# Exchanging two neighbouring stores in the DMA order of a matmul-and-subtract kernel

## The chip, the cores and the metric

The kernel runs on one core of a Trainium2 chip. The metric is device time in microseconds of one execution. The kernel before has a median of 210.92 us in four runs (210.59 to 211.15). Times inside a run are counted from the start of the profiled span, which is about 2 us shorter than the measured time of that same run. A transfer is spread over 16 DMA engines and leaves 16 landing records in the trace; "it lands" means the last of them, unless the first is named.

## The reference

```python
batch, m, k, n = 16, 512, 1024, 768
def reference(x, weight, sub_value):          # all float32
    return (np.matmul(x, weight) - sub_value).astype(np.float32)
```

The kernel sees it as 8192 rows of x by 1024, cut into 64 m tiles of 128 rows. Traffic with memory is 87 MB: 33.6 MB of x, 3.1 MB of weight, 25.2 MB of sub_value in, and 25.2 MB of result out.

## The kernel before

Every transfer is issued by the sync engine (SP), in the order of one list. A row ('x', 24, 8) loads m tiles 24 to 31 of x, 's' loads sub_value, 'o' stores the result. x has a ring of 16 slots; sub_value and the result share a ring of 32, and the subtraction works in place.

```python
SEGMENTS = [(0, 1), (1, 7)] + [(at, 8) for at in range(8, 64, 8)]
NX, NSO = 16, 32
TRANSFERS = [
    # ... cut: x and sub_value up to tile 15, all of the weight
    ('x', 16, 2), ('x', 18, 6), ('s', 16, 8),
    ('x', 24, 8), ('o', 0, 1), ('o', 1, 7), ('s', 24, 8), ('x', 32, 8), ('s', 32, 8), ('x', 40, 8),
    ('o', 8, 8), ('o', 16, 8), ('s', 40, 8), ('x', 48, 8), ('s', 48, 8), ('x', 56, 8),
    ('o', 24, 8), ('o', 32, 8), ('s', 56, 8), ('o', 40, 8), ('o', 48, 8), ('o', 56, 5),
    ('o', 61, 2), ('o', 63, 1),
]
```

What a row waits for, cut to the lines that matter. These waits stand on SP, which goes through its list in order:

```python
if kind == "x" and need:      # the slots' former tiles must have been cast
    waits.append((counter["cast"], max(cast_at[t] for t in need)))
    # ... cut
if kind == "s":               # the slots' former results must have landed in memory
    for t in need:
        waits.append(landed["o", t])
        # ... cut
if kind == "o":               # the tiles must have been subtracted
    waits.append((counter["finish"], max(finish_at[t] for t in need)))
    # ... cut
sem, value = lane((kind, at))  # the first semaphore whose former transfers are known to be over
```

A tile goes through ScalarE (cast to 16 bits), TensorE or VectorE (transposition), TensorE (16 matmuls of 128x384), and VectorE (the subtraction). The results of the matmuls have three buffers, so the matmuls of tile t need the subtraction of tile t - 3.

## Time and profile before

| | before |
|---|---|
| time, median of 4 | 210.92 us |
| span of the profiled run | 208.9 us |
| TensorE busy | 196.7 us, 94% |
| DMA engines' time in the transfers' queue | 97.7% |
| 49 to 186 us: TensorE busy, and rate of transfers | 136.72 of 137 us, 430 GB/s |

Two resources are full at once. Two more places bear on the argument and were not shown in it. First, TensorE's timeline of before at 186 us (start, duration, engine, line, what):

```profile
185.83 0.81 PE L198 MATMUL po_b<-w_sb,xtp_b 128*128 128x384 f16 x4
186.48 0.27 PE L335 MATMUL pt_b<-ident,x_b 128*128 128x128 f32 x1
186.75 0.81 PE L198 MATMUL po_b<-w_sb,xtp_b 128*128 128x384 f16 x4
```

Groups of four matmuls otherwise follow one another every 0.76 us; here the step is 0.92, a gap of 0.16 us that no list of waits names. VectorE's line for the subtraction of tile 56 ends 0.05 us before those matmuls (185.74 + 0.96 = 186.70, the first of three in the line):

```profile
185.74 2.69 DVE L417 TENSOR_TENSOR so_ring<-po_b,so_ring 128x768 f32<-128x768 f32 x3 [3.35 <-DMA so_ring<-in_sub_value_dram]
```

The second place is the last two stores of before, by size and time from issue to landing:

```profile
out_dram<-so_ring SPq DMA_DIRECT2D x1, 768.0 KB, 7.0
out_dram<-so_ring SPq DMA_DIRECT2D x1, 384.0 KB, 5.3
```

The last store, 384 KB, needs 5.3 us. Moving 384 KB at 430 GB/s takes 0.9.

### The profile page before, as it was taken

How to read it: one execution, taken by the hardware profiler on the slowest of the kernel's cores; microseconds unless marked ns; L12 is line 12 of the kernel's file. 1: busy time of each engine (PE TensorE's matmuls, PEld its weight loads, DVE VectorE, ACT ScalarE, POOL GpSimd, SP SyncE). 2: the span in 40 equal slices, each digit the busy share in tenths (PEclk: the TensorE clock that was granted, in tenths of full speed). 3: DMA queues.
4: the chain of work that ended last, by engine and by line, in shares of the span. 5: the costliest groups of instructions: out<-in, count | busy, mean ns of one | idle time of the engine just before them, and what ended most of it. 6: DMA issues, size and time to landing. Idle time of an engine off the chain costs nothing.

```text
span 208.9 us, 2614 instructions
## 1 busy us (share of the span) xinstructions
PE 196.7 (94%) x1234; PEld 75.4 (36%) x700; DVE 127.8 (61%) x224; ACT 108.8 (52%) x113; POOL 1.0 (0%) x7
## 2 busy tenths in 40 slices
PE   6999799989999999999999999999999999999950
PEld 0234244333434434433443443343344344334310
DVE  2323316955993995596499299369749929943330
ACT  4364768507664671762844767173584655525300
POOL 1000000000000000000000000000000000000000
PEclk9999999999999999999999999999999999999996
DMA  6999999999999999999999999999999999999992
GB/s 238 406 426 433 440 420 436 449 431 430 433 458 414 353 446 445 446 414 411 475 419 422 438 414 438 461 425 422 431 447 397 436 442 438 414 438 442 411 417 119
DMA packets 5620, 87.08 MB, mean 417 GB/s; under 512 B 624, under 2 KB 624, under 8 KB 2032
## 3 DMA queue, kind: packets, MB, share of 16 engines
q1 hardware_dynamic: 5616, 87.03, 97.7%
q8 instruction: 1, 0.02, 0.0%
q14 instruction: 3, 0.02, 0.0%
HBM read 61.87 MB, written 25.17 MB: 417 GB/s over the span
## 4 chain that ended last, share of the span: by engine, by line
PE 72%; DMA 18%; SPq 4%; ACT 1%; issue 1%; DVE 0%
PE po_b L198 65%; DMA x_ring<-in_x_dram 18%; PE pt_b L335 7%; SPq L298 3%; SPq L262 1%; ACT xt_b L348 0%; DVE so_ring L417 0%; ACT x_b L317 0%; SPq L553 0%; ACT x16p_b L317 0%; SPq L138 0%
## 5 line engine op out<-in xcount | busy, mean ns | idle before, releaser
L198 PE MATMUL po_b<-w_sb,xt_b 128*128 128x384 f16 x704 | 126.0, 326 | 0.3 <-ACT xt_b L348 0.2
L417 DVE TENSOR_TENSOR so_ring<-po_b,so_ring 128x768 f32<-128x768 f32 x64 | 60.4, 956 | 58.6 <-PE po_b L198 37.4
L348 ACT COPY xt_b<-pt_b 128x1024 f16<-128x1024 f16 x44 | 44.5, 1012 | 64.2 <-PE pt_b L335 63.2
L368 DVE STREAM_TRANSPOSE xtp_b<-x16p_b 32x256 f32<-32x256 f32 x144 | 62.7, 435 | 3.3 <-ACT x16p_b L317 1.1
L198 PE MATMUL po_b<-w_sb,xtp_b 128*128 128x384 f16 x320 | 61.4, 326 | 1.0 <-DVE xtp_b L368 0.9
L397 PEld LDWEIGHTS <-xt_b 128*128 128x128 f16 x352 | 34.4, 98 | 57.7 <-issue 53.6
L317 ACT CAST x_b<-x_ring 128x1024 f16<-128x1024 f32 x46 | 47.2, 1048 | 4.3 <-DMA x_ring<-in_x_dram 4.3
L335 PE MATMUL pt_b<-ident,x_b 128*128 128x128 f32 x184 | 47.6, 274 | 1.6 <-ACT x_b L317 1.4
L335 PEld LDWEIGHTS pt_b<-ident,x_b 128*128 128x128 f32 x184 | 25.3, 141 | 46.0 <-issue 41.3
L317 ACT CAST x16p_b<-x_ring 128x1024 f16<-128x1024 f32 x18 | 18.8, 1046 | 16.8 <-DMA x_ring<-in_x_dram 16.8
L397 PEld LDWEIGHTS <-xtp_b 128*128 128x128 f16 x160 | 15.7, 98 | 19.9 <-issue 17.8
L265 DVE CAST w_sb<-so_ring 128x768 f16<-128x768 f32 x8 | 4.1, 556 | 11.4 <-DMA so_ring<-in_weight_dram 11.4
L198 PE MATMUL po_b<-idle_x,idle_w 128*128 128x512 f16 x26 | 8.8, 495 | 1.7 <-POOL idle_x L178 1.7
L348 ACT COPY xtp_b<-pt_b 128x1024 f16<-128x1024 f16 x2 | 2.0, 1012 | 2.1 <-PE pt_b L335 2.1
L317 ACT ACT_TABLE_LOAD x1 | 1.3, 1283 | 0.9 <-SPq L138 0.9
L427 PEld LDWEIGHTS <-idle_w 128*128 128x128 f16 x4 | 0.4, 99 | 1.7 <-POOL idle_x L178 1.7
L187 DVE TENSOR_TENSOR ident<-along,across 32x32 f32<-32x32 f32 x4 | 0.7, 183 | 0.1
L179 DVE MEMSET ones<- 128x32 f32 x1 | 0.1, 85 | 1.0 <-SPq L138 1.0
L178 POOL MEMSET idle_x<- 128x512 f16 x1 | 0.5, 528 | 0.0
L499 ACT CAST stub<-ident 128x1 f16<-128x1 f32 x2 | 0.4, 195 | 0.0
L184 DVE STREAM_TRANSPOSE across<-along 128x32 f32<-128x32 f32 x1 | 0.2, 212 | 0.0
L476 POOL MEMSET mark<- 128x1 f32 x1 | 0.1, 99 | 23.6 <-ACT xtp_b L348 23.6
(7 smaller groups left out, 1.0 us busy)
## 6 DMA issues: line engine op xcount, KB each, us to landing
so_ring<-in_sub_value_dram SPq DMA_DIRECT2D x7, 3072.0 KB, 24.2
x_ring<-in_x_dram SPq DMA_DIRECT2D x5, 4096.0 KB, 23.8
out_dram<-so_ring SPq DMA_DIRECT2D x6, 3072.0 KB, 29.2
x_ring<-in_x_dram SPq DMA_DIRECT2D x2, 2048.0 KB, 27.0
so_ring<-in_weight_dram SPq DMA_DIRECT2D x4, 768.0 KB, 8.2
x_ring<-in_x_dram SPq DMA_DIRECT2D x1, 3072.0 KB, 28.6
out_dram<-so_ring SPq DMA_DIRECT2D x1, 2688.0 KB, 26.5
x_ring<-in_x_dram SPq DMA_DIRECT2D x2, 1024.0 KB, 24.8
```

Of the source, the lines that this page charges most:

```text
L178: pool.add(lambda: nc.gpsimd.memset(idle_x, 0.0), then=count("idle"))
L187: dve.add(lambda here=here: nc.vector.tensor_tensor(out=ident[here, here], in0=along[here], in1=across[here], op=mybir.AluOpType.is_equal, ...
L198: return nc.tensor.add_instruction(mybir.InstMatmult(name=nc.get_next_instruction_name(), engine=full.engine, ins=list(full.ins), outs=lis ...
L262: sp.add(lambda st=st, at=at: nc.sync.dma_start(out=st, in_=w_c[at]), then=(sem, 16))
L265: lambda at=at, r=r, st=st: nc.vector.tensor_copy(out=w_sb[:, at, r], in_=st[:, r]),
L298: sp.add(lambda here=here, there=there: nc.sync.dma_start(out=here, in_=there), waits, (sem, 16))
L317: act.add(lambda: nc.scalar.copy(out=to, in_=x_in), waits, count("cast"))
L335: pe.add(lambda: nc.tensor.transpose(words, from_, ident), waits, count("turn") if last else None)
L348: act.add(lambda: nc.scalar.copy(out=to, in_=pt_b[:, b]), waits, count("evac"))
L368: dve.add(lambda: nc.vector.transpose(xt[b * Q : (b + 1) * Q, :, a * Q : (a + 1) * Q], x16[a * Q : (a + 1) * Q, :, b * Q : (b + 1) * Q],), ...
L397: pe.add(lambda weights=weights: nc.tensor.ldweights(weights, tile_position=(0, 0)), [w for w in waits if w[0] in ready])
L417: dve.add(lambda: nc.vector.tensor_tensor(out=o, in0=po[:, :, :NS], in1=o, op=mybir.AluOpType.subtract), [landed["s", mi], (counter["mul"] ...
```

## The change

The store of tiles 1 to 7 goes ahead of the store of tile 0. The intent is that the large store starts as soon as it can; the bytes are the same.

```diff
-    ('x', 24, 8), ('o', 0, 1), ('o', 1, 7), ('s', 24, 8), ('x', 32, 8), ('s', 32, 8), ('x', 40, 8),
+    ('x', 24, 8), ('o', 1, 7), ('o', 0, 1), ('s', 24, 8), ('x', 32, 8), ('s', 32, 8), ('x', 40, 8),
```

## The prediction

> **What bounds the kernel now.** I read the page first for engine shares and the chain, then the DMA section, then the sync engine's timeline and waits around the two stores, and last what waits for the data that those stores gate. From the page, busy shares of a 208.9 us span, the DMA row in 40 slices, and the chain that ended last:
>
> ```profile
> PE 196.7 (94%) x1234; PEld 75.4 (36%) x700; DVE 127.8 (61%) x224; ACT 108.8 (52%) x113; POOL 1.0 (0%) x7
> ...
> DMA  6999999999999999999999999999999999999992
> ...
> PE 72%; DMA 18%; SPq 4%; ACT 1%; issue 1%; DVE 0%
> PE po_b L198 65%; DMA x_ring<-in_x_dram 18%; PE pt_b L335 7%; SPq L298 3%; SPq L262 1%; ACT xt_b L348 0%; DVE so_ring L417 0%; ACT x_b L317 0%; SPq L553 0%; ACT x16p_b L317 0%; SPq L138 0%
> ```
>
> The reader is to see two things. First, the chain is a transfer of x (18% of the span, in order of time the piece from 9.99 to 48.47 us) and then TensorE alone, from 49 us to the last subtraction at 201.26 us. Second, the DMA engines are full throughout as well: 87.08 MB at a mean of 417 GB/s. So the kernel has two near-bounds. A change of the order of transfers can only show if it changes what TensorE waits for after 49 us, or moves bytes after the end of the matmuls. After 50 us the matmul row's list of waits, asked for that stretch alone, has one entry:
>
> ```profile
> PE po_b L198 <- ACT xt_b L348: 0.2, 1, 0.2
> ```
>
> (columns: total us, times, longest). TensorE is idle for 0.2 us of the last 150 us of matmuls. There is nothing to win by feeding it better after 50 us; there is only something to lose.
>
> Now the stores themselves. The sync engine's timeline from 54 to 96 us (start, duration, what):
>
> ```profile
> 54.22 0.33 SPq L298 DMA_DIRECT2D x_ring<-in_x_dram  x1
> 54.59 0.91 SPq L298 DMA_DIRECT2D out_dram<-so_ring  x2
> 55.81 0.34 SPq L298 DMA_DIRECT2D so_ring<-in_sub_value_dram  x1
> 70.44 0.33 SPq L298 DMA_DIRECT2D x_ring<-in_x_dram  x1
> 81.54 0.33 SPq L298 DMA_DIRECT2D so_ring<-in_sub_value_dram  x1
> 94.80 0.33 SPq L298 DMA_DIRECT2D x_ring<-in_x_dram  x1
> ```
>
> These are x tiles 24 to 31, the two stores (one merged row), sub_value 24 to 31, x 32 to 39, sub_value 32 to 39, x 40 to 47. The two stores go out back to back at 54.59 and 55.07. Neither waits for a subtraction: the loading of x 24 to 31 ahead of them had waited for a cast until 54.22. Their sizes and landings, from the DMA issues of 54.5 to 55.5 us:
>
> ```profile
> out_dram<-so_ring SPq DMA_DIRECT2D x1, 2688.0 KB, 26.5
> out_dram<-so_ring SPq DMA_DIRECT2D x1, 384.0 KB, 20.6
> ```
>
> So tile 0 lands at 54.59 + 20.6 = 75.2 us and tiles 1 to 7 at 55.07 + 26.5 = 81.5 us. The one thing that waits for either is the load of sub_value 32 to 39, which overwrites the same slots of the ring. The sync engine's waits between 60 and 90 us:
>
> ```profile
> SPq L298 <- ACT x_b L317: 14.3, 1, 14.3
> SPq L298 <- DMA out_dram<-so_ring: 6.3, 1, 6.3
> SPq L59 <- DMA out_dram<-so_ring: 4.4, 1, 4.4
> ```
>
> After issuing x 32 to 39 (done at 70.77) it waits 4.4 us in a separate wait (line 59) for tile 0, to 75.2, then 6.3 us at the load itself for tiles 1 to 7, to 81.5. Only the later of the two landings matters.
>
> **What the Trainium skill says.** "DMA: Bandwidth & Descriptors", section "Queues, rings and completion order", says that each DMA engine consumes descriptors in ring order, and that one issuing engine has one ring on each of the 16. This case's trace agrees: all big transfers are in one queue (q1, 97.7% of the engines' time), and in the packet records each engine finishes its 32768-byte packets of x 24 to 31, then moves its 3072-byte packets of tile 0, then its 21504-byte ones of tiles 1 to 7. The landing records (last of 16 engines) follow the order of issue: x at 74.20, tile 0 at 75.16, tiles 1 to 7 at 81.52, sub_value 24 to 31 at 88.75, x 32 to 39 at 98.47, sub_value 32 to 39 at 105.73. The same page's "Anatomy of one DMA" says that DMA engines do not wait on semaphores, the issuing sequencer does. The waits above, on SP's queue, agree. So to exchange the two issues is to exchange two neighbours in a first-in first-out line.
>
> **The change part by part.**
> It adds and removes no instruction. The number of bytes, packets and their sizes stay; the two rows of the queue change places.
>
> 1. Issue. Tiles 1 to 7 now go out first and wait for the subtraction of tile 7, which tile 0 did not need. That subtraction is long done: the subtraction of tile 8 began at 46.14 us, when its sub_value landed (46.05), and the vector engine goes in order, so tile 7 was done at least 8.4 us before 54.59. Tile 0 behind it needs no wait any more. An already met wait costs no time that the trace shows: the two issues take 0.91 us together now, and I expect 0.91 again. Cost 0.0 us; sub_value 24 to 31 is again issued at 55.8.
>
> 2. Landing. Tile 0's share of the queue is 75.16 - 74.20 = 0.96 us (384 KB at 430 GB/s gives 0.91). Tiles 1 to 7 therefore land about 0.96 us earlier, at 80.6 (26.0 us after an issue at 54.59), and tile 0 lands last at about 81.5 (26.5 us after 55.07), 6.3 us later than now. The later of the two stays at 81.5, since the sum of bytes ahead of it is the same; I allow 0.3 us either way for which of the 16 engines is last (one transfer's landings spread over 2.3 to 2.7 us).
>
> 3. The gate. Tile 0's wait is still the first in program order, so the separate wait grows from 4.4 to about 10.8 us, and the one at the load (6.3 us) is met on arrival and vanishes. 4.4 + 6.3 = 10.7 before, 10.8 after. The load of sub_value 32 to 39 is issued at 81.5 to 81.9, at most 0.1 us later for passing two instructions after the event instead of one.
>
> 4. What that load is worth. When issued at 81.54 it stands behind x 32 to 39, which lands at 98.47. So a delay of the issue by a few tenths does not move its landing at 105.7. And it isn't needed then: the subtraction of tile 32 starts at 113.03 (I count back eight rows from the one at 137.33, which waited 4.66 us for sub_value 40 to 47 landing at 137.24), 7.3 us later. Off the path: 0.0 us.
>
> 5. The semaphores. The program gives each transfer the first free semaphore. By reading that logic, tile 0's and tiles 1 to 7's (the seventh and the ninth) are exchanged, both are free again at the same later point, and every later transfer keeps its own. No wait is added at the end.
>
> Sum: 0.0 + 0.0 + 0.0 us on the path, so 210.76 us stays; I write 210.8.
>
> **The rivals.** (a) The first store is held up by tile 7 and holds the queue behind it. For it: SP goes in order, and sub_value 24 to 31 behind it lands at 88.75, with its first use at 89.19, only 0.44 us later. Against it: the 8.4 us of margin in step 1. Even a hold-up of 1 us would not reach TensorE: the late sub_value at 137.33 stalled the vector engine for 4.66 us, and the matmul row shows no wait for it. It would make 210.8 to 211.
> (b) The last landing moves, since small packets now come at the end: a lone late engine could hold the gate. For it: the spread of 2.3 to 2.7 us. Against: 7.3 us of slack in step 4, and the line of x 32 to 39 before it. The load could be issued some 7 us late and still be in time, by estimate. It makes 210.8.
> (c) It gets faster, since the large store starts 0.96 us sooner. For it: DMA is at nine tenths everywhere. Against: nothing waits for tiles 1 to 7 without tile 0, and the end is set by TensorE. A gain would have to come from another run of chance: 210.6.
> (d) The switch from loads to stores costs differently with a large packet first. Tile 0's packets take 0.121 us for 3072 bytes (25.4 GB/s an engine), tiles 1 to 7's 0.799 us for 21504 (26.9): in either order the sum is the same, and a tenth of a microsecond at 75 us would be absorbed as above.
>
> **Range and chances.** The three runs of before lie between 210.59 and 211.15, so 0.56 us is the scatter of one and the same kernel. As every step gives zero, the range is that scatter with a little more for another chip or hour: 210.2 to 211.4. Within 2% means 206.5 to 215.0; no rival comes near either end. Chance of same 0.985; slower 0.01, for a queue effect that I cannot see here; faster 0.005.
>
> **What would show each step.** Step 1: two issues from about 54.6, together 0.9 us, no wait for the vector engine. Step 2: 2688 KB landing about 26 us after issue, 384 KB about 26.5 (20.6 before). Step 3: the separate wait of the sync engine for a store about 10.8 us, the 6.3 us one gone, the sub_value load issued at 81.5 to 81.9. Step 4: the landing of sub_value 32 to 39 at 105.7 within some tenths, the subtraction of tile 32 at about 113.0, and a chain still of x, then TensorE. It would be wrong if the two stores were issued later than 55.5, if the later of the two landed after 83 us, or if matmuls after 50 us showed waits for a subtraction.

## The result

The changed kernel takes 210.98 us (210.84 to 211.06, four runs), the kernel before 210.92. The ratio is 1.0003, with an interval of 0.9986 to 1.0021: the same. The instructions of TensorE, VectorE, ScalarE and GpSimd are the same ones in the same order; only the two neighbours in SP's list differ.

SP's timeline of the changed kernel, from 54 us to the load of sub_value 32 to 39:

```profile
54.42 0.33 SPq L298 DMA_DIRECT2D x_ring<-in_x_dram  x1
54.79 0.91 SPq L298 DMA_DIRECT2D out_dram<-so_ring  x2
56.01 0.34 SPq L298 DMA_DIRECT2D so_ring<-in_sub_value_dram  x1
70.64 0.33 SPq L298 DMA_DIRECT2D x_ring<-in_x_dram  x1
81.80 0.33 SPq L298 DMA_DIRECT2D so_ring<-in_sub_value_dram  x1
```

Everything is where it was, 0.2 to 0.3 us later throughout, because already x 24 to 31 went out 0.2 us later (54.42 against 54.22), ahead of the first changed instruction. The two stores by size and time to landing, and SP's waits between 60 and 90 us (total, times, longest):

```profile
out_dram<-so_ring SPq DMA_DIRECT2D x1, 2688.0 KB, 26.0
out_dram<-so_ring SPq DMA_DIRECT2D x1, 384.0 KB, 26.5
```

```profile
SPq L298 <- ACT x_b L317: 14.3, 1, 14.3
SPq L59 <- DMA out_dram<-so_ring: 10.8, 1, 10.8
```

Tile 0 now lands last, 26.5 us after issue instead of 20.6. The separate wait has grown from 4.4 to 10.8 us, and the 6.3 us wait at the load itself is gone. The load goes out 11.16 us after the one of x before it, against 11.10 before (81.54 - 70.44).

The chain of the page looks quite different, and that is a trap. Shares of the span by engine:

```profile
PE 51%; DMA 40%; ACT 3%; DVE 1%; issue 1%; POOL 0%; SPq 0%; POOLq 0%; DVEq 0%; ACTq 0%
```

DMA has gone from 18% to 40% in a kernel that takes as long. The chain in order of time, 140 to 188 us, shows the new way that it takes (start, duration, what):

```profile
140.40 31.17 DMA out_dram<-so_ring
...
171.58 14.43 DMA so_ring<-in_sub_value_dram
...
186.11 0.97 DVE so_ring L417
...
187.12 0.81 PE po_b L198 x4
```

The store of tiles 24 to 31 lands, the load of sub_value 56 to 63 follows it into the same slots, tile 56 is subtracted, and the matmuls of tile 59 begin. That was so before as well, with the gap of 0.16 us shown above. After, the gap is 0.33 (187.12 against the 186.79 of the regular step), and now the timeline names it:

```profile
187.12 0.81 PE L198 MATMUL po_b<-w_sb,xtp_b 128*128 128x384 f16 x4 [0.17 <-DVE so_ring L417]
```

The chain follows the one thing that came last. Where two come within some tenths of a microsecond of each other, it tips from one to the other and carries 22% of the span with it. The exchange did not tip it: after_again below is the changed kernel, unedited, and its page has yet another chain:

```profile
PE 75%; DMA 13%; DVE 6%; SPq 3%; issue 1%; DVEq 0%
```

### The profile page after: what moved, and what is told of

Read it like the earlier page. It is cut to its first block, busy times and chain, and to the rows that moved or that the text cites. A ratio compares the mean times of both kernels' runs of the same rounds, so it can differ in the third digit from the quotient of the medians.

```text
span 209.2 us, 2614 instructions
## 1 busy us (share of the span) xinstructions
PE 196.1 (94%) x1234; PEld 75.4 (36%) x700; DVE 127.8 (61%) x224; ACT 108.9 (52%) x113; POOL 1.0 (0%) x7
## 4 chain that ended last, share of the span: by engine, by line
PE 51%; DMA 40%; ACT 3%; DVE 1%; issue 1%; POOL 0%; SPq 0%; POOLq 0%; DVEq 0%; ACTq 0%
PE po_b L198 46%; DMA x_ring<-in_x_dram 19%; DMA out_dram<-so_ring 15%; DMA so_ring<-in_sub_value_dram 7%; PE pt_b L335 5%; ACT xt_b L348 1%; ACT x_b L317 1%; DVE so_ring L417 1%; POOL idle_x L178 0%; SPq L298 0%; POOL idle_w L177 0%; POOLq L553 0%; ACT x16p_b L317 0%; DVEq L59 0%; ACTq L59 0%
## 5 line engine op out<-in xcount | busy, mean ns | idle before, releaser
L317 ACT CAST x16p_b<-x_ring 128x1024 f16<-128x1024 f32 x18 | 18.8, 1046 | 17.1 <-DMA x_ring<-in_x_dram 17.1
L198 PE MATMUL po_b<-idle_x,idle_w 128*128 128x512 f16 x26 | 8.2, 469 | 1.7 <-POOL idle_x L178 1.7
```

Of the source, the lines that this page charges most:

```text
L198: return nc.tensor.add_instruction(mybir.InstMatmult(name=nc.get_next_instruction_name(), engine=full.engine, ins=list(full.ins), outs=lis ...
L317: act.add(lambda: nc.scalar.copy(out=to, in_=x_in), waits, count("cast"))
```

## The experiments

All are made from the changed kernel, and all ratios are to the kernel before. Letters of theories run on through the experiments: A is that the transfers are one first-in first-out line in which an issue is free as long as the line has work; E is that this line sets the end, F that TensorE does.

**after_again.** The changed kernel, unedited.

> The changed kernel again, on the chip that the next three share, to have its scatter beside theirs. Both theories: 211.0 us, ratio to the kernel before 0.998 to 1.002. If the small difference of the first measurement (210.98 against 210.92) were real, the ratio would stay above 1.000 in all rounds; I expect it to go either way.

Measured: 210.78 us, before 210.78; ratio 1.0005 (0.9991 to 1.0018). Nothing to explain. Both kernels moved by 0.1 to 0.2 us between sessions, more than the 0.06 us by which they had differed.

**gate_mid.** How late may the gate of sub_value 32 to 39 (SP's wait for the landing of both stores) open?

```diff
-    ('x', 24, 8), ('o', 1, 7), ('o', 0, 1), ('s', 24, 8), ('x', 32, 8), ...
+    ('x', 24, 8), ('o', 1, 7), ('s', 24, 8), ('o', 0, 1), ('x', 32, 8), ...
```

> Tile 0's store goes one place further back, behind the load of sub_value 24 to 31. Theory A (the transfers are a first-in first-out line, and an issue is free as long as the line has work ahead of it): tile 0 lands at about 88.9 us instead of 81.6, the load of sub_value 32 to 39 is issued at about 89 instead of 81.8, but it stands behind x 32 to 39 (landing 98.5) all the same and lands at about 105.9 as now. Time 211.0, within 0.3. Rival B (the later a gate opens, the later its load lands): landing 7.3 us later, at 113, just when it is needed, and x 40 to 47 unchanged; up to 0.5 us more.

Measured: 210.9 us, ratio 1.0003 (0.9988 to 1.0019). From SP's timeline:

```profile
70.92 0.33 SPq L298 DMA_DIRECT2D x_ring<-in_x_dram  x1
89.06 0.33 SPq L298 DMA_DIRECT2D so_ring<-in_sub_value_dram  x1
```

The load goes out at 89.06 instead of 81.80, and by the trace's landing records it lands at 105.9, as in the changed kernel. Its 7.3 us of later issue were spent standing in a line that was 7.3 us shorter. A holds, B falls.

**gate_late.** Tile 0's store goes behind x 32 to 39, so that the gate opens only when the line has run empty.

```diff
-    ('x', 24, 8), ('o', 1, 7), ('o', 0, 1), ('s', 24, 8), ('x', 32, 8), ('s', 32, 8), ...
+    ('x', 24, 8), ('o', 1, 7), ('s', 24, 8), ('x', 32, 8), ('o', 0, 1), ('s', 32, 8), ...
```

> Tile 0's store goes two more places back, behind x 32 to 39. Theory A: it lands last in the line, at about 98.6, and only then the load of sub_value 32 to 39 goes out, when the line is empty; that leaves a hole of about 2 us in the transfers (the first load of the kernel, on an empty line, landed its first bytes about 2.9 us after issue, of which about 1.2 are its own moving), so sub_value 32 to 39 lands at about 108, and all later transfers 1.5 to 2.5 us later. Sub_value 56 to 63, which the tile-59 matmuls already wait for by 0.2 to 0.3 us, comes later by as much. Time 212.5 to 213.5, ratio 1.007 to 1.012. Rival C (TensorE sets the time after 49 us and a late transfer is absorbed by slack): 211.0.

Measured: 215.58 us, ratio 1.0232 (1.0216 to 1.0248). C falls: nothing absorbs it. The direction is that of A, the size is 4.8 us where I had given 1.5 to 2.5. Stretches of 5 us of this run (time, busy of each engine, clock, DMA share, GB/s):

```profile
90.00:95.00 5.00, 5.00 (x34) 1.77 (x18) 4.83 (x11) 2.90 (x3) 0.00 (x0) 1.00 0.93 399
95.00:100.00 5.00, 5.00 (x34) 1.94 (x18) 2.61 (x5) 1.04 (x1) 0.00 (x0) 1.00 0.47 143
100.00:105.00 5.00, 5.00 (x35) 2.17 (x20) 2.89 (x5) 4.71 (x5) 0.00 (x0) 1.00 0.83 344
```

In the changed kernel the middle stretch moves 410 GB/s. The store landed on the first of the 16 DMA engines at 96.0 and on the last at 98.7; the wait is for the last, and the next load, issued at 98.77, lands on the first engine at 107.9 and on the last at 108.8. Less its own 7.3 us of moving, the last engine stood still for 2.8 us and the first for 4.6. I had sized the hole for an engine that finishes with the last. The load is 2.9 us late by its last landing, and x 40 to 47 behind it 4.3 us (119.9 against 115.6): another 1.4 us, which go with slowed packets (26 of those of x 40 to 47; by the packet records they lengthen its moving by 1.1 us on the mean engine), told under s24_first. The last landing is 4.6 us later than in the changed kernel.

**hold15.** The rival (a) of the prediction at full size: the first store waits for a later tile.

```diff
-  waits.append((counter["finish"], max(finish_at[t] for t in need)))
+  waits.append((counter["finish"], 16 if at == 1 else max(finish_at[t] for t in need)))
```

> The first store is held until the subtraction of tile 15 instead of tile 7 (ends at about 63.5 us instead of before 46), so the two stores and the load of sub_value 24 to 31 are issued at about 63.5 to 64.8 instead of 54.7 to 55.9, a hold-up of 8.9 us of the issuing engine. Theory A: the line still has x 24 to 31 before it until 74.3, so the landings stay as they are (80.7, 81.6, 88.9) within some tenths; 211.0 us, within 0.3. Rival D (an issue held up holds up what comes behind it, my rival a at full size): landings about 8.9 us later, sub_value 24 to 31 at about 97.8, tile 27 waits and the time grows by several us, to 214 or more.

Measured: 211.06 us, ratio 1.0008 (0.9993 to 1.0023). The issues of 63 to 65 us and their times to landing:

```profile
so_ring<-in_sub_value_dram SPq DMA_DIRECT2D x1, 3072.0 KB, 24.4
out_dram<-so_ring SPq DMA_DIRECT2D x1, 2688.0 KB, 17.1
out_dram<-so_ring SPq DMA_DIRECT2D x1, 384.0 KB, 17.6
```

The large store goes out 8.9 us later (63.68 against 54.79) and needs 8.9 us less (17.1 against 26.0). D falls.

**hold19.** As hold15 with 20 in place of 16, so that the hold outlasts the work in the line.

> The first store is held until the subtraction of tile 19, which ends at about 76.7 us, after x 24 to 31 has landed (74.3) and the line is empty. Theory A: the line stands still from about 72 to 74 until the first bytes of the store, about 2 us after 76.7; all landings from the stores on come 4 to 5 us later (stores at about 85 and 86, sub_value 56 to 63 at about 190), and the matmuls of tile 59 wait for that long. Time 214.5 to 216.5, ratio 1.017 to 1.026. Rival C (slack absorbs it): 211.0. Rival D (a hold-up counts in full from 54.7 on, 22 us): above 220.

Measured: 217.55 us, ratio 1.0324 (1.0309 to 1.0339). C and D fall; of A the mechanism holds and the size is again too small. Five microseconds of this run in which nothing moved:

```profile
72.00:77.00 5.00, 5.00 (x34) 1.86 (x18) 4.85 (x9) 2.98 (x4) 0.00 (x0) 1.00 0.00 0
```

By the landing records tile 0's store is 4.5 us late (86.3 against 81.7), as expected, and sub_value 32 to 39 4.9; x 40 to 47 is 5.7 us late, with slowed packets again, and the last landing 6.2.

Both late experiments lengthen the line, so both E and F allow them. The next runs tell E and F apart.

**tail_plain, tail_pe6, tail_pe12, tail_pe24.** TensorE's work is lengthened near the end, with the transfers as they are. tail_plain is the control and has the change of LOOP alone: TensorE's program is a loop of ten rounds of six tiles, and with nine the last six tiles are written out, so that one of them can be changed.

```diff
-LOOP = (4, 6, 10)
+LOOP = (4, 6, 9)
+  for _ in range(24 if mi == 62 and c == 0 and r == 0 else 0):     # 6, 12 or 24
+      pe.add(lambda weights=weights: loaded_matmul(
+          po[:, 0, :NS], weights, w_sb[:, 0, 0, :NS], start=True, stop=True), waits)
+      waits = []
```

> Control for the next two: the last six tiles of TensorE's loop are written out, nothing else. Both theories: 211.0 us, within 0.3.

> As tail_plain, with 6 more matmuls of 0.163 us before those of tile 62 (their result is overwritten, the outputs stay right): TensorE ends 0.98 us later. Theory E (the line of transfers, full to the end, sets the end: the last store is issued at 202.5 and its landings follow those of the stores before it): the line has work until about 206.9, so the last landing stays at 207.8; 211.0 us, within 0.3. Theory F (the chain as the profile tells it, TensorE sets the end): 212.0.

> As tail_plain, with 12 more matmuls before those of tile 62, so TensorE ends 1.95 us later. Theory E with a slack of about 2.9 us: 211.0, within 0.3. Theory F, or a slack below 1.5: 211.5 to 212.9.

> As tail_plain, with 24 more matmuls of 0.163 us before those of tile 62: TensorE ends 3.9 us later and the last store is issued at about 206.4. Theory E: the line empties at about 207 (the store of tiles 61 and 62 is issued at about 203.8 and lands by about 207), and the last store lands about 3.3 us after its issue, at about 209.7 instead of 207.8; so 212.5 to 213.2. Theory F: 214.9.

| | us, median | ratio (interval) | last subtraction starts | last store: issue to landing |
|---|---|---|---|---|
| tail_plain | 210.85 | 0.9994 (0.9981 to 1.0007) | 201.50 | 5.3 |
| tail_pe6 | 210.86 | 1.0006 (0.9991 to 1.0021) | 202.63 | 4.0 |
| tail_pe12 | 210.84 | 1.0003 (0.9989 to 1.0017) | 203.37 | 3.4 |
| tail_pe24 | 211.81 | 1.0052 (1.0039 to 1.0065) | 205.44 | 2.3 |

The last two stores of tail_pe12 and of tail_pe24, by size and time to landing:

```profile
out_dram<-so_ring SPq DMA_DIRECT2D x1, 768.0 KB, 5.1
out_dram<-so_ring SPq DMA_DIRECT2D x1, 384.0 KB, 3.4
```

```profile
out_dram<-so_ring SPq DMA_DIRECT2D x1, 768.0 KB, 3.2
out_dram<-so_ring SPq DMA_DIRECT2D x1, 384.0 KB, 2.3
```

TensorE can end almost 2 us later and the time doesn't move; the last store just stands less long behind others. With 3.94 us (205.44 - 201.50) the time grows by 0.96, so the slack of TensorE at the end is about 3.0 us. F falls. My size for tail_pe24 was off, and the time lies below the range that I had given: I had taken 3.3 us for a store on an empty line, from the first load of the kernel, and it needs 2.3.

**short_s56.** The line is made shorter, with TensorE's work as it is. The result is wrong (relative error 0.25): tiles 60 to 63 subtract stale data.

```diff
+            if kind == "s" and at == 56:
+                here, there = here[:, :4], there[:, :4]
```

> Wrong result on purpose: the last load of sub_value brings tiles 56 to 59 only, 1.57 MB less (3.65 us of the line at 430 GB/s), and the tiles 60 to 63 subtract what lies in the ring. TensorE has the same work. Theory E (the line of transfers sets the end, TensorE ends with about 2.9 us of slack, from the 3.9 us delay that cost 1.0): the last landing moves forward until the last store lands 2.3 us after its issue (as with the 24 added matmuls); with the matmuls of tile 59 no longer waiting, about 0.3 us more. Time 207.4 to 208.4, ratio 0.984 to 0.989. Theory F (TensorE sets the end): at most those 0.3 us, 210.6.

Measured: 207.87 us, ratio 0.9864 (0.9849 to 0.9879). The last two stores:

```profile
out_dram<-so_ring SPq DMA_DIRECT2D x1, 768.0 KB, 3.2
out_dram<-so_ring SPq DMA_DIRECT2D x1, 384.0 KB, 2.3
```

The last subtraction starts at 201.65, no earlier than in the changed kernel (201.63), and yet the time is 2.9 us shorter: the slack that the added matmuls had measured. The load is shorter by 3.65 us of moving; the last 0.7 are kept by TensorE, which now does set the end, as the last store's bare 2.3 us show. E holds from both sides.

One thing has to be added about the end of the line. Before, the last store lands on the first of the 16 DMA engines at 204.91 us and on the last at 207.59, and after 204 us few engines still move anything (DMA share and GB/s are the last two columns):

```profile
204.00:210.00 6.00, 0.00 (x0) 0.00 (x0) 0.00 (x0) 0.00 (x0) 0.00 (x0) 0.56 0.20 81
```

On the first engine the store needs 2.66 us from its issue, against 2.10 on the idle line of tail_pe24 (206.43 to 208.53, the last engine at 208.70). So most of TensorE's 3.0 us of slack is the backlog of the engines that finish last; against the engine that finishes first it is about 0.6 us, by estimate. What sets the end is the line of the latest engines. Why some run late was not tested.

**s24_first.** Both stores go behind sub_value 24 to 31.

```diff
-    ('x', 24, 8), ('o', 1, 7), ('o', 0, 1), ('s', 24, 8), ('x', 32, 8), ...
+    ('x', 24, 8), ('s', 24, 8), ('o', 1, 7), ('o', 0, 1), ('x', 32, 8), ...
```

> The load of sub_value 24 to 31 goes ahead of both stores. Two questions. First, the gate opens at about 89 instead of 81.6, as with tile 0's store alone moved; the line hides it: no cost. Second, the stall at the first change from loads to stores (the packets of x 24 to 31 took up to 1.9 us instead of 1.21, some 1.5 us of the line): if it comes from loads of x being overtaken by stores, it is gone or moves to the end of sub_value 24 to 31. If it goes, the line and the time are 1.0 to 1.5 us shorter, 209.5 to 210; if it only moves, 211.0 within 0.3. I expect that it moves.

Measured: 211.05 us, ratio 1.0014 (1.0002 to 1.0027). So this order costs 0.14%, by the interval 0.27% at the most, and whether that little is real stays open; the stall has only moved. In the changed kernel 28 of the 34 packets of x that start between 68 and 73 us take longer than 1.3 us, up to 2.78, where 1.21 is usual; in s24_first none does, and there 29 of the 50 packets of sub_value that start between 75 and 80 us take more than 1.0 us, up to 1.94, where 0.91 is usual. Windows of s24_first around it (DMA share and GB/s are the last two columns):

```profile
74.00:76.00 2.00, 2.00 (x15) 0.73 (x7) 1.93 (x6) 1.00 (x2) 0.00 (x0) 1.00 0.94 406
76.00:78.00 2.00, 2.00 (x15) 0.59 (x6) 1.94 (x4) 2.00 (x4) 0.00 (x0) 1.00 1.21 381
78.00:80.00 2.00, 2.00 (x14) 0.59 (x6) 1.73 (x3) 0.85 (x1) 0.00 (x0) 1.00 0.81 338
```

The number varies from run to run (16 in before, 20 in after_again). The slowed packets are the last loads ahead of the first store. In hold19, where no store followed x 24 to 31 in time, its packets are all at 1.21 us (maximum 1.213), and those of x 40 to 47, ahead of the next stores, are slowed instead (28 of 128, up to 2.04). In gate_late both are. Why the later changes from loads to stores in the changed kernel show none of it stays open.

No version beat both kernels. The kernel that is faster computes something else.

## Why the prediction was right, and where its reasons were not

- **Step 1, issue:** right. Two stores in 0.91 us, with no wait for VectorE. hold15 shows that more than the claimed margin protects it: even a wait that is not met, and holds the issue up by 8.9 us, is free.
- **Step 2, landing:** right to the tenth, 26.0 and 26.5 us. The line is first-in first-out; gate_mid and hold15 show it with other orders.
- **Step 3, the gate:** right. 4.4 and 6.3 us of waits became one of 10.8.
- **Step 4, what the load is worth:** right. It lands 7.3 us ahead of its use (105.9, subtraction of tile 32 at 113.24), and gate_mid opened the gate 7.3 us later for nothing. Its sign "a chain still of x, then TensorE" did not come (DMA 40%), but after_again, the same kernel, has another chain again, so that this sign could not test the step.
- **Step 5, semaphores:** right. The seventh and the ninth are exchanged, and the later ones are unchanged in the trace.
- **What bounds the kernel:** the part of the reasoning that failed. "There is nothing to win by feeding it better after 50 us" looked at TensorE alone, and rival (c) said "the end is set by TensorE". The tail runs and short_s56 show that the line sets the end and TensorE has about 3 us of slack at the end. The exchange is free not because TensorE hides it, but because the line has the same bytes and no hole. The forecast of zero survived since both reasons give zero; as far as it rested on this one, that was luck.
- **Rival (a):** its conclusion was right, its second argument wrong. It took sub_value 40 to 47 as the proof that lateness is absorbed ("Even a hold-up of 1 us would not reach TensorE"). The load that counts is sub_value 56 to 63: the matmuls of tile 59 already stood 0.16 us for it before, and 0.33 after. What absorbs a hold of the issue is the line's backlog; what lengthens the line is not absorbed, as gate_late (4.8 us) and hold19 (6.7 us) show.
- **The sign of being wrong** that I had named, a wait of the matmuls for a subtraction after 50 us, did appear. The list of waits for the matmuls after 50 us:

```profile
PE po_b L198 <- ACT xt_b L348: 0.2, 1, 0.2
PE po_b L198 <- DVE so_ring L417: 0.2, 1, 0.2
```

It is not caused by the exchange: after_again, the same kernel, does not have it, and its matmuls of tile 59 start without any gap (186.99, 0.76 after 186.23). Of the edited runs with tile 0's store behind the other, gate_mid has it (0.4 us), while hold15, s24_first and tail_plain do not, though the gap itself is there in hold15 and s24_first (0.24 and 0.20 us) as it was before. It is the tie of line and TensorE, tipping with tenths of a microsecond from run to run. My sign was too sharp for a kernel with two bounds.

The Trainium skill, "Perfetto Trace Analysis", section "Identifying the Most-Contended Engine", warns that the busy share of the matmuls is a poor measure of the distance to the limit, since pipelined matmuls look smaller in the trace, and says to look at the use of memory for DMA. No run here tests that reason or that advice. Another reason for care: TensorE was 94% busy and yet had 3 us of slack where it counted.

## What to carry to other kernels

Where transfers form one full first-in first-out line, as here, reordering neighbours or issuing later costs next to nothing until the line runs empty; ask of each change whether it makes a hole, and size the hole for each DMA engine, not only for the one that finishes last (2.8 us on the last and 4.6 on the first in gate_late). When two resources are both near 100%, the profile's chain can name whichever came last by tenths of a microsecond, and another in the next run of the same kernel: find the true bound by lengthening one, then shortening the other, near the end. A last store that takes several times its own moving time to land is a sign that it stood in a line, here above all in that of the late engines.

## What the Trainium skill lacked or had wrong

- "DMA: Bandwidth & Descriptors", section "Anatomy of one DMA", gives a fixed cost of about 2.0 us and a fit (2.0 us and the bytes at 436 GB/s) for the path through GpSimd, and has no such figure for transfers issued by SP. For stores issued by SP on an idle line, these runs show 2.3 us for 384 KB and 3.2 us for 768 KB; the page's fit, as an estimate, gives 2.9 and 3.8.
- The same page, section "Queues, rings and completion order", says that an engine takes its descriptors in order, and warns that completion is not first-in first-out per issuing engine; in all 13 traces here the 39 transfers landed in the order of issue. It does not have what waiting for a landing costs an otherwise full line: in gate_late the 16 engines landed the store 2.7 us apart, and the hole was 2.8 us on the last engine and 4.6 on the first.
- The same page, section "Where 436 GB/s comes from", says that the memory side, some 358 GB/s, binds transfers between HBM and SBUF. That sentence misleads for a program on one core: loads and stores mixed ran at 430 GB/s here from 49 to 186 us, near the 435 that the same section gives as the ceiling of the fabric. The page's own table for loads with one core (425 GB/s) agrees with that; it has no figure for loads and stores mixed.
- I found no page that has the slowing of the last loads ahead of the first store: packets of 32 KB took up to 2.78 us instead of 1.21.
